# Two projection pairs of a gated-recurrence block: two of eight chunks by Strassen's scheme

## The chip, the cores and the metric

The kernel runs on one core of a Trainium2 chip. The metric is the device time of one execution in microseconds. A core has TensorE (PE in the profile, its weight loads PEld), VectorE (DVE), ScalarE (ACT), GpSimd (POOL), and queues for transfers that SyncE (SP) issues here. Each engine works through one queue in a fixed order, and waits for what other engines or transfers must have finished.

## The reference

One layer of a decoder block on 256 tokens of 2048 features, in fp32. Its first part is a projection of the normalized input, whose columns are cut into ten fields, each of them used in its own way:

```python
h = rmsnorm(x, norm_mix_g[i])
u = h @ w_in[i]                       # 2048 -> 12288
c_g, b_g, xa, za, q, fl, iv, og, ga, gb = jnp.split(u, split_idx, axis=-1)
ya = b_g * causal_dwconv3(c_g * xa, conv_w[i]) * jax.nn.silu(za)
...                                   # log_f and kk from fl
o = hgrn2_chunked(silu(q), kk, iv, log_f)      # a gated linear recurrence, 8 heads of 128
o = o * lax.rsqrt(jnp.mean(o * o, axis=-1, keepdims=True) + EPS)
yb = (o * hg_norm_g[i]) * jax.nn.silu(og)
m = jax.nn.sigmoid(ga) * (ya @ w_a_out[i]) + jax.nn.sigmoid(gb) * (yb @ w_b_out[i])
x = x + m @ w_o[i]
gate = jax.nn.sigmoid(rmsnorm(x, ple_norm_g[i]) @ w_ple_gate[i])
x = x + gate * (p[i] @ w_ple_proj[i])
return rmsnorm(x, final_norm_g)
```

The fields c, b, xa, za, q, f, iv and og are 1024 columns wide each, ga and gb 2048.

## The kernel before

**Numbers.** All products are made from fp32 values that are cut into a high part (hi, type fp32r) and the rest (lo). A product is three matmuls: hi by hi, hi by lo, lo by hi. The weights are cut on the chip: a transfer brings a chunk into a tile `raw` (three of them, line 106), ScalarE copies it to `whi` (line 151), VectorE subtracts to get `wlo` (line 152). `whi` and `wlo` are pairs of buffers, four in the pool `wp`. Such a pair is given back when PE has read it.

**Steps.** The work of PE is one list of steps (`steps`, line 181; `pos` is the step's number). A step takes one chunk of weights: 256 input features by 512 columns, so 128 x 1024 values in the tile. In a plain step both halves of a chunk meet both halves of the tokens, which makes 4 products, 12 matmuls of 512 columns (line 1147). A group of 8 steps makes 512 columns of a field. The columns of the projection go in two halves j = 0 and 1, and in each half the groups come in the order f, q, iv, og, c, xa, za, b (line 37). Ahead of them stand four steps for the projection of p, behind them the gates ga and gb with the output products A and B, then O, and last the gate PG of the last part. q of the first half is steps 12 to 19, iv 20 to 27.

**Strassen's scheme where it is used already.** The gates of j = 1 to 3 are taken in pairs (groups "GG", with the list `GATES`, line 42), and so is a pair of PG ("GP", with `LATE`). An entry (g, c) of such a list is two plain steps, chunks c and c + 1 of the pair's group g. An entry ("S", c) is a joint chunk: chunk c of both groups at once, in four parts. `combine_weights` (line 159) makes the sums and differences of the two groups' weights on VectorE, four parts are split, the second of them from the tile t2, half as wide, and `pair_products` (line 1157) makes seven products of 512 columns instead of the eight of two plain steps. It needs sums and differences of x as well, the forms (`forms` and `forms_of_x`, lines 722 to 757): xT is loaded once more for these chunks, scaled with the norm's gain, added on VectorE, split, and kept in tiles. PE gathers the results in eight PSUM banks, four named g and four s; `sums` (line 765) puts them together with six half-wide additions and one wide one on VectorE and one copy on ScalarE, as a generator that starts when the first joint chunk does.

**Epilogues.** What follows a group is a generator in `active`, and each step of PE's list moves every generator on by one (`advance`, line 1130). A half's f is evicted with the norm's scale (`scaled`, line 306), written to DRAM in four transfers, read back in one, and transposed on VectorE (`turned`, line 285); then come two sigmoids, four logarithm calls and a scan (lines 341 to 388). q is a sigmoid and a product in PSUM, turned in the same way (line 392). iv is one scaled eviction, og a sigmoid and a product, and behind og the recurrence `hgrn` of this half begins. The norm of x comes from squares of the tokens (`load_tokens`, `add_squares`, `norm_of_x`, lines 1033 to 1053), which are loaded from step 10 on and squared from step 13; so the f of the first half waits for it until step 17 (line 1241).

**What sets the order.** A scheduler writes the order of every engine's queue when the program is built; an instruction for a later step can stand ahead of one for an earlier step there. `issue_after` asks for a place behind the last split, and `keep_in_program_order` keeps a few instructions where the program has them. `ahead` (line 1138) says how many steps the splits are made ahead of PE: three, and one more where a stretch has additional buffers (`more`, line 207: pool `tmp2` around the gates; every fifth step takes its pair from there, line 140).

**Memory.** `tmp1` is the pool of the two halves: eight work tiles, the tiles v, qT, kT, b and og, and for the recurrence a pair X and the tiles a, both and aoff (line 430 and the lines behind it). yaT holds the turned result of branch A, one half of the tile for each j.

Of the kernel before, what the change touches and what calls it, by code (L numbers as in the profile page):

```python
# [9 lines left out]
F32 = mybir.dt.float32  # L10
F32R = mybir.dt.float32r
# [4 lines left out]
P = 128  # L16
# [7 lines left out]
CW = 512  # L24
# [15 lines left out]


GATES = ("S", 0), (0, 2), ("S", 1), (1, 2), ("S", 4), (0, 6), ("S", 5), (1, 6)
LATE = (0, 4), ("S", 0), (0, 6), ("S", 1), (1, 4), ("S", 2), ("S", 3), (1, 6)


# [6 lines left out]
def hybrid_kernel(ctx, tc, xT, x, pT, prm, gfin, masks, w_in, w_a, w_b, w_o, w_pg, w_pp, out):  # L52
# [10 lines left out]
    pools, closers = {}, {}  # L63
# [13 lines left out]
    state = {"tmp": "tmp1"}  # L77
# [3 lines left out]
    def nm(s):  # L81
        uid[0] += 1
        return f"{s}_{uid[0]}"
# [17 lines left out]
    half = {}  # L101
# [28 lines left out]
    def split(pos, c0=0, c1=2 * CW):  # L130
        part = part_of[pos]
        src = load(pos)[:, part % 2, :]
        if joint[pos]:

            src = load(pos)[:, part == 3, :]
            if part == 1:
                src, c1 = half[unit_of[pos]], CW

        pool, n = (pools["late"], 6) if (pos - state.get("late", len(steps))) % 10 < 6 and "late" in state else (wp, 4)
        if more(pos) and pos % (4 + MORE) < MORE:  # L140
            pool, n = pools[more(pos)], MORE
        if pos not in parts:
            parts[pos] = tuple(
                pool.tile([P, 2 * CW], F32R, tag=tag, bufs=n, name=nm(tag)) for tag in ("whi", "wlo")
            )
        hi, lo = parts[pos]
        s = slice(c0, c1)
        with ExitStack() as order:
            for i in state["before"].pop() if state.get("before") else ():
                order.enter_context(tc.issue_after(i))  # L150
            a = nc.scalar.activation(out=hi[:, s], in_=src[:, s], func=AF.Copy)  # L151
            v = nc.vector.tensor_tensor(  # L152
                out=lo[:, s], in0=src[:, s], in1=hi[:, s].bitcast(F32), op=ALU.subtract
            )
        state["splits"] = (a.ins, v.ins)
        if joint[pos] and part == 0:
            combine_weights(pos)

    def combine_weights(pos):

        b = load(pos).rearrange("p i (k c) -> p (i k) c", k=2)
        t2 = half[unit_of[pos]] = pools["tmp2" if pos in gates else "tmp3"].tile([P, CW], F32, tag="t2", bufs=2 if pos in gates else 1, name=nm("t2"))
        nc.vector.tensor_tensor(  # L163
            out=b[:, 0:4:3, :], in0=b[:, 0:3:2, :], in1=b[:, 3:4, :].to_broadcast([P, 2, CW]), op=ALU.subtract
        )
        nc.vector.tensor_tensor(out=t2, in0=b[:, 2, :], in1=b[:, 0, :], op=ALU.add)  # L166
        nc.vector.tensor_tensor(out=b[:, 1, :], in0=b[:, 1, :], in1=t2, op=ALU.subtract)
# [35 lines left out]
    of_kind = lambda *kinds: [pos for pos, (gi, c) in enumerate(steps) if groups[gi][0] in kinds]  # L203
    gates, late = of_kind("GG"), of_kind("PG")[0]
    gates = range(gates[0] - 12, gates[-1] + 9)

    def more(pos):

        return "tmp2" if pos in gates else None

    TOKENS, NORM = 10, 13
    FIRST = 6

    praw = t4()[:, : 2 * T]
# [180 lines left out]
        plain_times(psum, sg, qt)  # L395
        state["qT", j] = yield from turned(qt, 5, t4("qT", 1))

    def ep_iv(j, psum):
        v = t4("v", 1)
        scaled(psum, v)  # L400
        state["v", j] = v
        yield
# [316 lines left out]
        yield  # L719


    def forms(op, pool, tag, r, chunks):
# [11 lines left out]
        hi, lo = (pool.tile([P, 1024], F32R, tag=tag + x, bufs=len(chunks) // 2, name=nm(tag + x)) for x in "hl")  # L734
# [7 lines left out]
    def forms_of_x():  # L742

        joined = sorted(c for u, c in GATES if u == "S")
        for n in range(0, len(joined), 2):
            chunks = joined[n : n + 2]
            raw = t4()
            r = raw.rearrange("p (u k t) -> p u k t", u=2, k=2)
            for u in range(2):
                nc.sync.dma_start(out=r[:, u], in_=xT[:, 2 * chunks[u] : 2 * chunks[u] + 2, :])  # L750
            for u in range(2):
                yield
                for k in range(2):
                    h = r[:, u, k, :]
                    nc.scalar.activation(out=h, in_=h, func=AF.Identity, scale=gain(PRM_GMIX, 2 * chunks[u] + k))
            yield
            yield from forms("hT", pools["tmp2"], f"Sx{n}", r, chunks)
            yield

    def add(out, x, y):  # L760
# [32 lines left out]
    def ep_pair(j, e, left):  # L793
# [42 lines left out]
    def ep_o(j, psum):  # L836
# [18 lines left out]
        if j < 2:  # L855
# [8 lines left out]
            yield from forms("x1T", pools["tmp3"], f"So{j}", r, (2 * j, 2 * j + 1))  # L864
# [342 lines left out]
    for pos, (gi, c) in enumerate(steps[:last_group]):  # L1207
# [36 lines left out]
        if program:  # L1244
# [45 lines left out]
        if c == nch - 1:  # L1290
# [3 lines left out]
            if kind == "ga" and j == 0:  # L1294
                finish()
                second_part()
                active.append(forms_of_x())
# [106 lines left out]
```

## Time and profile before

Three runs took 815.71, 815.15 and 814.84 us, the median is 815.15.

| | |
|---|---|
| profiled execution | 814.94 us |
| its span on the core | 813.1 us |
| granted TensorE clock, mean | 0.997 |
| matmuls | 4196 |
| memory read | 173.97 MB |
| mean transfer rate over the span | 231 GB/s |

The span begins with the first instruction and ends with the last; what lies around it is 814.94 - 813.1 = 1.8 us. Times in the profile are microseconds from the start of the span. A row of the timeline is: start, busy time, engine, line, operation, result <- operands, number of instructions that were taken together, and in brackets an idle time before it and who ended it. A row of the groups is: busy time, count, share or idle time. L1147 is line 1147 of the kernel that is printed above, and tiles go by their names in it (the operand names begin with the result, so `wlo<-raw,whi` is a split's second half). A matmul shows 0.39 us from issue to end, but the next one is issued before that end.

### The profile page before, as it was taken

The numbers are of one execution on the slowest core, as the hardware profiler recorded it, in microseconds if no ns is written. First come the engines' busy times: TensorE is split into PE (matmuls) and PEld (weight loads), VectorE is DVE, ScalarE is ACT, GpSimd is POOL, SyncE is SP. The second block draws the span as 40 slices with busy tenths as digits, with TensorE's granted clock in tenths as the row PEclk, the third lists the DMA queues.
The fourth block names the chain that finished last, engine by engine and source line by source line (L and its number), as shares of the span: only waits on it lengthen the run. The fifth ranks groups of instructions, "written<-read, shape, count | busy, mean of one in ns | idle before, by whom it ended". The sixth has DMA issues, their size and how long they took to land.

```text
span 813.1 us, 10989 instructions
## 1 busy us (share of the span) xinstructions
PE 802.5 (99%) x4196; PEld 666.9 (82%) x4196; DVE 629.6 (77%) x742; ACT 465.2 (57%) x609; POOL 91.1 (11%) x74
## 2 busy tenths in 40 slices
PE   9999999999999999999999999999999999999995
PEld 7888888888888888888888888888888888888875
DVE  5747697967766488967767998998997657779996
ACT  7667475555555465565664555564564456665653
POOL 1000045400000055200001000100100000001012
PEclk9999999999999999999999999999999999999998
DMA  9979656747767555647764774774766687887442
GB/s 337 366 281 338 226 172 206 228 172 237 258 233 256 186 183 202 213 156 264 269 238 148 224 272 144 248 257 157 259 236 230 213 300 257 283 315 252 165 181 105
DMA packets 46709, 188.33 MB, mean 232 GB/s; under 512 B 5312, under 2 KB 14784, under 8 KB 31552
## 3 DMA queue, kind: packets, MB, share of 16 engines
q1 hardware_dynamic: 46512, 187.36, 66.6%
q8 instruction: 33, 0.54, 0.3%
q10 hardware_dynamic: 144, 0.26, 0.1%
q14 instruction: 20, 0.16, 0.1%
HBM read 173.97 MB, written 13.63 MB: 231 GB/s over the span
## 4 chain that ended last, share of the span: by engine, by line
PE 90%; DVE 5%; DMA 1%; issue 1%; ACT 1%; POOL 0%; ACTq 0%; POOLq 0%; DVEq 0%
PE g L1147 73%; PE g L1169 11%; PE s L1169 4%; DVE wlo L152 2%; DMA raw<-in_w_pg 1%; PE s L1147 1%; PE s L450 1%; DVE t L911 1%; DVE raw L163 1%; DMA raw<-in_w_pp 0%; DVE xs L912 0%; ACT whi L151 0%; DVE t L929 0%; DVE t L761 0%; DVE t L166 0%
## 5 line engine op out<-in xcount | busy, mean ns | idle before, releaser
L152 DVE TENSOR_TENSOR wlo<-raw,whi 128x1024 fp32r<-128x1024 f32 (+1 forms) x311 | 385.1, 1254 | 154.3 <-ACT whi L151 153.0
L151 ACT ACTIVATE whi<-raw 128x1024 fp32r<-128x1024 f32 (+1 forms) x311 | 320.8, 1049 | 251.1 <-PE g L1147 195.6
L1147 PE MATMUL g<-whi,xh 128*128 128x512 f32 (+1 forms) x656 | 251.8, 385 | 0.6 <-DVE t L761 0.6
L1147 PE MATMUL g<-wlo,xh 128*128 128x512 f32 (+1 forms) x656 | 251.9, 384 | 0.0
L1147 PE MATMUL g<-whi,xl 128*128 128x512 f32 (+1 forms) x656 | 251.7, 384 | 0.0
L1147 PEld LDWEIGHTS g<-whi,xh 128*128 128x128 f32 x656 | 123.3, 188 | 25.2 <-DVE t L761 1.0
L1147 PEld LDWEIGHTS g<-whi,xl 128*128 128x128 f32 x656 | 123.3, 188 | 24.5
L1147 PEld LDWEIGHTS g<-wlo,xh 128*128 128x128 f32 x656 | 123.3, 188 | 24.2
L1169 PE MATMUL g<-wlo,xh 128*128 128x512 f32 x160 | 62.2, 389 | 0.0
L1169 PE MATMUL g<-whi,xl 128*128 128x512 f32 x160 | 62.2, 389 | 0.0
L1169 PE MATMUL g<-whi,xh 128*128 128x512 f32 x160 | 62.1, 389 | 0.0
L1147 PE MATMUL g<-whi,mh 128*128 128x512 f32 x128 | 49.8, 389 | 0.0
L1147 PE MATMUL g<-wlo,mh 128*128 128x512 f32 x128 | 49.8, 389 | 0.0
L1147 PE MATMUL g<-whi,ml 128*128 128x512 f32 x128 | 49.6, 389 | 0.0
L151 ACT ACTIVATE whi<-t 128x512 fp32r<-128x512 f32 x16 | 10.1, 630 | 53.7 <-DVE t L166 53.7
L1169 PEld LDWEIGHTS g<-whi,xh 128*128 128x128 f32 x160 | 30.0, 188 | 6.2
L1169 PEld LDWEIGHTS g<-wlo,xh 128*128 128x128 f32 x160 | 30.0, 188 | 6.2
L1169 PEld LDWEIGHTS g<-whi,xl 128*128 128x128 f32 x160 | 30.0, 188 | 6.2
L824 POOL TENSOR_TENSOR t<-ga,gb 128x512 f32<-128x512 f32 x6 | 10.6, 1780 | 193.0 <-issue 118.1
L1147 PE MATMUL g<-whi,yaTh 128*128 128x512 f32 (+1 forms) x74 | 28.0, 385 | 0.5 <-ACT whi L151 0.5
L1147 PEld LDWEIGHTS g<-whi,mh 128*128 128x128 f32 x128 | 24.0, 188 | 5.0
L1147 PEld LDWEIGHTS g<-wlo,mh 128*128 128x128 f32 x128 | 24.0, 188 | 5.0
(250 smaller groups left out, 931.4 us busy)
## 6 DMA issues: line engine op xcount, KB each, us to landing
raw<-in_w_in SPq DMA_DIRECT2D x73, 1024.0 KB, 4.9
raw<-in_w_in SPq DMA_DIRECT2D x34, 512.0 KB, 6.0
raw<-in_w_o SPq DMA_DIRECT2D x16, 1024.0 KB, 6.0
raw<-in_w_pg SPq DMA_DIRECT2D x12, 1024.0 KB, 6.1
turn<-t SPq DMA_DIRECT2D x72, 128.0 KB, 2.6
t<-turn SPq DMA_DIRECT2D x18, 512.0 KB, 5.1
raw<-in_w_a SPq DMA_DIRECT2D x8, 1024.0 KB, 5.3
raw<-in_w_b SPq DMA_DIRECT2D x8, 1024.0 KB, 5.4
```

Of the source, the lines that this page charges most:

```text
L151: a = nc.scalar.activation(out=hi[:, s], in_=src[:, s], func=AF.Copy)
L152: v = nc.vector.tensor_tensor(out=lo[:, s], in0=src[:, s], in1=hi[:, s].bitcast(F32), op=ALU.subtract)
L163: nc.vector.tensor_tensor(out=b[:, 0:4:3, :], in0=b[:, 0:3:2, :], in1=b[:, 3:4, :].to_broadcast([P, 2, CW]), op=ALU.subtract)
L450: nc.tensor.matmul(heads(bk)[r, h, c if at is None else slice(at, at + 32)], key(h)[:, r], query(h)[:, c], start=True, stop=True, tile_pos ...
L824: (nc.vector if j == 3 else nc.gpsimd).tensor_tensor(out=spread(m, t), in0=blocks(ga[:, s]), in1=blocks(gb[:, s]), op=ALU.add)
L911: nc.vector.tensor_tensor(out=gt[:, s], in0=gt[:, s], in1=pw[:, s], op=ALU.mult)
L1147: nc.tensor.matmul(psum, a, b, start=first and n == 0, stop=last and n == 2)
L1169: nc.tensor.matmul(banks[name], x, y[:, s], start=k == total[name] and i == 0, stop=k == 1 and i == 2)
```

## The change

Two pairs of groups become joint groups: q and iv of the first half ("QV") and iv and og of the second ("VG"). In each, chunks 0 and 1 of the eight are joint, in the order of the new list `INNER`, and the other six of both groups stay plain. Steps 12 to 31 are now QV, everything behind stands four steps later, and behind VG eight.

- The forms of x for chunks 0 and 1 are made at step 9 (`FORMS`). They are kept in the second half of the two yaT tiles, which is free until branch A of the second half. Both pairs use the same forms; the gates keep theirs, which are made later.
- For the steps of both pairs, from three ahead of them on, every fifth step takes its weight buffers from the pair X of `tmp1`, and t2 is one of the tiles both and aoff. The splits go one step further ahead there.
- `ep_inner` puts the banks together with `sums` and then starts the epilogues of the two groups on the result in SBUF, in place of PSUM.
- The loads of the tokens are asked for in the branch for pairs too, since steps 12 and 13 are now there.

```diff
+INNER = (0, 2), (0, 4), ("S", 0), (0, 6), ("S", 1), (1, 2), (1, 4), (1, 6)
...
+        tags = "whi", "wlo"
         if more(pos) and pos % (4 + MORE) < MORE:
             pool, n = pools[more(pos)], MORE
+            if more(pos) == "tmp1":
+                tags, n = ("X", "X"), 2
...
+        pool, tag, n = ("tmp2", "t2", 2) if pos in gates else ("tmp3", "t2", 1)
+        if more(pos) == "tmp1":
+            pool, tag, n = "tmp1", ("both", "aoff")[unit_of[pos] // 2 % 2], 1
+        t2 = half[unit_of[pos]] = pools[pool].tile([P, CW], F32, tag=tag, bufs=n, name=nm("t2"))
...
-        if j == 0 or kind not in ("ga", "gb"):
+        if (kind, j) in (("q", 0), ("iv", 1)):
+            groups.append(({"q": "QV", "iv": "VG"}[kind], j, w_in, n, "hT", INNER))
+        elif (kind, j) in (("iv", 0), ("og", 1)):
+            continue
+        elif j == 0 or kind not in ("ga", "gb"):
             groups.append((kind, j, w_in, n, "hT"))
...
+    inner = [range(at[0] - 3, at[-1] + 1) for at in (of_kind("QV"), of_kind("VG"))]
...
-        return "tmp2" if pos in gates else None
+        return "tmp2" if pos in gates else "tmp1" if any(pos in at for at in inner) else None
 
-    TOKENS, NORM = 10, 13
+    TOKENS, NORM, FORMS = 10, 13, 9
...
-    def ep_iv(j, psum):
-        v = t4("v", 1)
+    def ep_iv(j, psum, v=None):
+        v = t4("v", 1) if v is None else v
...
+    def ep_inner(kinds, j, e, left):
+
+        def then(q, g):
+            halves = [g[:, A], g[:, B]]
+            after = ep_iv(j, halves, g) if kinds[q] == "iv" else epilogues[kinds[q]](j, halves)
+            next(after)
+            active.append(after)
+
+        yield from sums(e, left, lambda: tuple(t4("v", 1) if k == "iv" else t4() for k in kinds), then)
...
+        if pos == FORMS:
+            held = [x[:, 4:, :].rearrange("p k t -> p (k t)") for x in state["yaT"]]
+            active.append(forms_of_x(INNER, lambda n: lambda: held))
+            step(active[-1])
...
             if c == (min(n for n, (u, _) in enumerate(program) if u == "S"), 0):
-                active.append({"GG": ep_pair, "GP": ep_gates_late}[kind](j, banks, left))
+                if kind in ("QV", "VG"):
+                    active.append(ep_inner({"QV": ("q", "iv"), "VG": ("iv", "og")}[kind], j, banks, left))
+                else:
+                    active.append({"GG": ep_pair, "GP": ep_gates_late}[kind](j, banks, left))
             pair_products(c, program, opname)
             ask_ahead()
+            if 0 <= pos - TOKENS < 4:
+                load_tokens(pos - TOKENS)
```

`forms` and `forms_of_x` take the list and a function that gives the tiles, and else do what they did. Lines of the changed kernel lie up to 35 further down than those of the kernel before.

More of the change, by code (lines that the diff above doesn't have):

```diff
@@ L139, in split @@
         pool, n = (pools["late"], 6) if (pos - state.get("late", len(steps))) % 10 < 6 and "late" in state else (wp, 4)
+        tags = "whi", "wlo"
         if more(pos) and pos % (4 + MORE) < MORE:
             pool, n = pools[more(pos)], MORE
+            if more(pos) == "tmp1":
+                tags, n = ("X", "X"), 2
         if pos not in parts:
             parts[pos] = tuple(
-                pool.tile([P, 2 * CW], F32R, tag=tag, bufs=n, name=nm(tag)) for tag in ("whi", "wlo")
+                pool.tile([P, 2 * CW], F32R, tag=tag, bufs=n, name=nm("w" + x)) for tag, x in zip(tags, ("hi", "lo"))
             )
@@ L161, in combine_weights @@
         b = load(pos).rearrange("p i (k c) -> p (i k) c", k=2)
-        t2 = half[unit_of[pos]] = pools["tmp2" if pos in gates else "tmp3"].tile([P, CW], F32, tag="t2", bufs=2 if pos in gates else 1, name=nm("t2"))
+        pool, tag, n = ("tmp2", "t2", 2) if pos in gates else ("tmp3", "t2", 1)
+        if more(pos) == "tmp1":
+            pool, tag, n = "tmp1", ("both", "aoff")[unit_of[pos] // 2 % 2], 1
+        t2 = half[unit_of[pos]] = pools[pool].tile([P, CW], F32, tag=tag, bufs=n, name=nm("t2"))
         nc.vector.tensor_tensor(
@@ L719, in ep_gb, with forms @@
         yield
-    def forms(op, pool, tag, r, chunks):
+    def forms(op, made, r, chunks):
         f = t4()
@@ L733, in forms @@
         yield
-        hi, lo = (pool.tile([P, 1024], F32R, tag=tag + x, bufs=len(chunks) // 2, name=nm(tag + x)) for x in "hl")
+        hi, lo = made()
         nc.scalar.activation(out=hi, in_=f, func=AF.Copy)
@@ L740, in forms, with form_tiles, forms_of_x @@
                 state["S", op, chunks[u], i] = hi[:, s], lo[:, s]
-    def forms_of_x():
-        joined = sorted(c for u, c in GATES if u == "S")
+    def form_tiles(pool, tag):
+        return lambda: tuple(pool.tile([P, 1024], F32R, tag=tag + x, bufs=1, name=nm(tag + x)) for x in "hl")
+    def forms_of_x(program, made):
+        joined = sorted(c for u, c in program if u == "S")
         for n in range(0, len(joined), 2):
@@ L756, in forms_of_x @@
             yield
-            yield from forms("hT", pools["tmp2"], f"Sx{n}", r, chunks)
+            yield from forms("hT", made(n), r, chunks)
             yield
@@ L863, in ep_o @@
             r = x1.rearrange("p (u k t) -> p u k t", u=2, k=2)
-            yield from forms("x1T", pools["tmp3"], f"So{j}", r, (2 * j, 2 * j + 1))
+            yield from forms("x1T", form_tiles(pools["tmp3"], f"So{j}"), r, (2 * j, 2 * j + 1))
             return
@@ L1296, in hybrid_kernel @@
                 second_part()
-                active.append(forms_of_x())
+                active.append(forms_of_x(GATES, lambda n: form_tiles(pools["tmp2"], f"Sx{n}")))
                 step(active[-1])
```

## The prediction

> **What bounds the kernel now.** I read the page's busy times first, then the chain that ended last, then the waits, then single stretches.
>
> ```profile
> span 813.1 us, 10989 instructions
> PE 802.5 (99%) x4196; PEld 666.9 (82%) x4196; DVE 629.6 (77%) x742; ACT 465.2 (57%) x609; POOL 91.1 (11%) x74
> PE 90%; DVE 5%; DMA 1%; issue 1%; ACT 1%; POOL 0%; ACTq 0%; POOLq 0%; DVEq 0%
> ```
> ```profile
> 16.70 119.68 PE g L1147 x528
> 547.20 21.76 PE g L1147 x96
> ```
> ```profile
> ACT whi L151 <- PE g L1147: 195.6, 129, 4.4
> PEld g L1147 <- DVE t L761: 1.0, 1, 1.0
> ```
>
> The chain is 90% PE. Its pieces give the price of a matmul: 119.68 / 528 = 21.76 / 96 = 0.2267 us. (A matmul's own row says 0.39 us: that is issue to end of a pipelined instruction, not its price.) The page's PE share alone would not prove that PE is the bound, but the waits do: ACT's splits stand 195.6 us waiting until PE gives a weight buffer back, and the one wait of PE's weight loads on DVE is 1.0 us. So time goes by the count of matmuls, as long as the splits keep ahead. They do by a margin that differs from place to place (columns: window, length, then busy us of PE, PEld, DVE, ACT, POOL, the granted clock, DMA share, GB/s):
>
> ```profile
> 40.00:60.00 20.00, 20.00 (x90) 16.57 (x89) 8.57 (x10) 12.17 (x17) 0.78 (x2) 1.00 0.73 293
> 60.00:80.00 20.00, 20.00 (x89) 16.54 (x89) 14.38 (x19) 13.90 (x17) 0.00 (x0) 1.00 0.94 324
> 240.00:260.00 20.00, 20.00 (x90) 16.56 (x89) 15.55 (x16) 11.12 (x13) 1.96 (x1) 1.00 0.75 253
> 260.00:280.00 20.00, 20.00 (x90) 16.54 (x89) 8.58 (x7) 9.42 (x10) 0.00 (x0) 1.00 0.61 206
> 460.00:480.00 20.00, 20.00 (x90) 16.57 (x89) 18.69 (x20) 12.75 (x14) 0.00 (x0) 1.00 0.63 225
> ```
>
> The first two windows hold q and iv of the first half, the next two iv and og of the second, the last a gate pair that is already done by Strassen: there DVE is 93% busy and PE still runs without a hole. The granted clock is 1.00 in all.
>
> The Trainium skill ("Perfetto Trace Analysis", section "Identifying the Most-Contended Engine") holds matmul busy time to be a bad measure and would judge TensorE's headroom by the busy share of its weight loads. That is 82% here, which read literally leaves 18% of room. But in every window above it is 16.5 of 20, also where nothing but matmuls runs, so 83% is what a full PE shows in this kernel, and I take PE as full.
>
> **The gain.** A Strassen chunk takes 7 products of three matmuls (21) where two plain parts take 24. Two chunks in each of two pairs: 12 matmuls fewer, 12 x 0.2267 = 2.72 us. That is all the change can give: 812.4 us.
>
> **What is added, and how much DVE has left.** Durations on DVE back to back, from a gate pair, with the scan and the copy of f's epilogue:
>
> ```profile
> 443.44 1.28 DVE L819 TENSOR_TENSOR gb<-gb,g 128x512 f32<-128x512 f32 x2
> 450.04 1.22 DVE L163 TENSOR_TENSOR raw<-raw 128x1024 f32<-128x1024 f32 x1
> 451.29 0.69 DVE L166 TENSOR_TENSOR t<-raw 128x512 f32<-128x512 f32 x1
> 452.02 0.69 DVE L167 TENSOR_TENSOR raw<-raw,t 128x512 f32<-128x512 f32 x1
> 452.77 0.69 DVE L152 TENSOR_TENSOR wlo<-t,whi 128x512 fp32r<-128x512 f32 x1
> 453.92 5.76 DVE L152 TENSOR_TENSOR wlo<-raw,whi 128x1024 fp32r<-128x1024 f32 x5 [0.47 <-ACT whi L151]
> 459.72 1.23 DVE L163 TENSOR_TENSOR raw<-raw 128x1024 f32<-128x1024 f32 x1
> ```
> ```profile
> 83.06 2.28 DVE L380 TENSOR_TENSOR_SCAN b<-carry,t 128x1024 f32<-128x1024 f32 x1
> 85.26 1.20 DVE L152 TENSOR_TENSOR wlo<-raw,whi 128x1024 fp32r<-128x1024 f32 x1
> 86.38 1.08 DVE L385 COPY tot<-b 128x8 f32<-128x8 f32 x1
> 87.37 0.15 DVE L386 TENSOR_TENSOR tot<-b,lfl 128x8 f32<-128x8 f32 x1
> ```
>
> One wide subtraction costs 5.76/5 = 1.15 and a half-wide one 0.64. A joint chunk needs 3 x 1.15 + 0.65 for its splits and 1.25 + 0.73 + 0.75 for the combination, 6.8 us, in 4.76 us of PE (21 matmuls); two plain parts need 2.3 in 5.44. The two chunks of a pair add about 9 us to DVE, the sums six half-wide additions and one wide (5 us), the forms of x some 3 us, once. So the first stretch (23 us busy in 40) comes to about 40 in 42, the second (24) to about 38 in 42. On average it fits; what decides is the order. I therefore took the built order of the changed kernel and summed each queue along it: every instruction starts when its queue is free and the tile or buffer that the program makes it wait for is there. The same sum over the first gate pair of the kernel as it is gives no hole in PE and meets DVE's starts above to 0.2 to 1.1 us, so I trust it to about half a microsecond per place.
>
> **The second pair (iv, og), from 240.98.**
>
> ```profile
> 240.98 0.39 PE L1147 MATMUL g<-whi,xh 128*128 128x512 f32 x1
> ```
>
> Counted from there, plain parts one to four end at 2.7, 5.4, 8.2 and 10.9; the first joint chunk ends at 15.6, the next two plain parts at 21.1. ACT's queue has the split of the first chunk's fourth part ahead of its second and third. This one uses the borrowed X pair, which the third plain part holds until 8.1, while DVE has finished the combination at 6.1 plus 0.6 and stands still until ACT's hi is there at 9.2. From 9.2 on DVE has in one row: three subtractions (1.15 + 0.6 + 1.15), f's scan (2.2), one more (1.15), the copies (1.06), two (1.15 + 1.27), the second combination (1.27 + 0.73 + 0.68), 0.6, q's transpose (1.3), and then the lo of the second chunk's third part (1.23): 24.8. PE wants it nine matmuls into that chunk, at 21.1 + 10 x 0.2267 = 23.35. **Stall: 1.45 us.** Nothing behind it is late again.
>
> **The first pair (q, iv), from 38.30.**
>
> ```profile
> 38.30 0.39 PE L1147 MATMUL g<-whi,xh 128*128 128x512 f32 x1
> ```
> ```profile
> 49.38 1.06 ACT L151 ACTIVATE whi<-raw 128x1024 fp32r<-128x1024 f32 x1 [1.66 <-PE g L1147]
> 50.35 1.04 ACT L1041 ACTIVATE t<-t 128x1024 f32<-128x1024 f32 x1
> 58.24 1.27 ACT L308 ACTIVATE t<-g,r1r 128x512 f32<-128x512 f32 x2 [1.32 <-POOL r1r L271]
> ```
>
> Here the built order of PE already pushes the products with forms of x behind plain ones. The hi of the forms stands on ACT behind a split that PE releases at 12.45 and a square of the tokens: 12.45 + 0.97 + 1.04 + 1.06 = 15.55 against 15.4 wanted; the lo follows by 1.25. About 0.3 us lost. The matmul that reads that lo also gives back the buffer for the second chunk's first split: 17.3 (with the 0.3), ACT 1.06, DVE 1.23, the combination 1.27 + 1.27 less the overlap + 0.73 + 0.6, and the fourth part's lo at 23.5; PE wants it at 22.3. Another 1.2, and 0.2 behind it. **Stall: 1.7 us.**
>
> **The first half's f.** Its epilogue needs the norm of x, whose squares now stand on ACT among the splits of the second chunk: eviction at about 62.8 instead of 58.24. Then f goes out to DRAM and back:
>
> ```profile
> 59.54 1.78 SPq L294 DMA_DIRECT2D turn<-t  x4
> 63.96 0.33 SPq L296 DMA_DIRECT2D t<-turn  x1
> ```
> ```profile
> t<-turn SPq DMA_DIRECT2D x1, 512.0 KB, 5.8
> ```
> ```profile
> 69.94 1.24 DVE L300 STREAM_TRANSPOSE t<-t 128x1024 f32<-128x1024 f32 x1
> ```
>
> 58.24 to 63.96 + 5.8 = 69.8 is 11.5 us, so about 74.4. DVE reaches that transpose at 73.4 and stands behind it; every split behind it waits too. ACT's two sigmoids, the two halves of q's sigmoid, the table load and three logarithms (5.5 us) come before og's first split, which is at 81.2, its lo at 83.5; PE wants it two matmuls into og, at 38.30 + 186 x 0.2267 + 1.7 + 0.45 = 82.6. **Stall: 0.9 us.** This is the least certain term: it is 0 with a lag of 10.5 us and 2 with 12.6. The ends are the two lags that the trace shows, 69.8 - 58.24 above and q's, which took 12.5 from 64.81 (first DMA of the turn) to 73.70 + 3.6 = 77.3 (the read's landing) behind f's:
>
> ```profile
> 64.81 3.20 SPq L294 DMA_DIRECT2D turn<-t  x4
> 73.70 0.34 SPq L296 DMA_DIRECT2D t<-turn  x1
> ```
> ```profile
> t<-turn SPq DMA_DIRECT2D x1, 512.0 KB, 3.6
> ```
>
> I take f's own, since the load between its parts is the same. The 512 KB of xT for the forms take the place of a token load in SP's queue, so S0's weights land as before and the tokens one load later; the squares alone wait for those. I cost it at 0, at worst 512 KB at the 324 GB/s of the second window above, 1.6 us. Also 0: the borrowed tiles X, both, aoff and the second half of yaT (hgrn's users of the first half end before the second pair, yaT's writer comes after it), the s banks (free in both stretches), and hgrn of the second half, whose y comes 2.7 us later on DVE while PE's order gives it 2.7 us more.
>
> **Sum.** -2.72 + 1.45 + 1.7 + 0.9 = +1.3 us. Against the profiled execution (814.94 us, its span 813.1) 816.2; the median of the runs shown is 815.15, which gives 816.4. 0.2% of it, 1.6 us, is about what a measurement of this kernel can tell from no change.
>
> **Rivals.**
> 1. Everything is hidden, as in the gate pairs: 812.4. For it: 18.69 of 20 busy on DVE at 460 to 480 without a hole. Against: there the parts are split in order, no scan, squares or transposes stand between them. It needs all three stalls to be wrong.
> 2. f's turn is in time (lag below 10.5), the two other stalls stay: 815.6.
> 3. Slower: f comes back from DRAM later than 74.4, because the 1 MB load that stands between its write and its read goes first. Each us beyond costs one us of PE; with q's lag, 12.5 and more, and token loads one place later, 2 to 3 us: 818 to 819. It decides from a lag of about 12.
> 4. PE was not the bound, and fewer matmuls give nothing back: the stalls would be hidden in that room as well or cost 4 us in full, up to 819. Waits of 195.6 us on PE speak against it. This is the way the skill's rule on weight loads would have it.
>
> **How the numbers follow.** Forecast (816.4) 0.44, rival 2 0.20, rival 3 0.23, rival 1 0.10, rival 4 0.03. The forecast's own range is 815.7 to 817.2, so a third of it lies above the 816.8 where "slower" begins; rivals 2 lies within, 3 and 4 are slower, 1 is faster: faster 0.10, same 0.50, slower 0.40. For 8 in 10 the range leaves out the far ends of rivals 1 and 3: 813.6 to 818.5.
>
> **What would show it.** PE's count falls by 12 matmuls. PE, now without a hole from 17 to 780, gets holes near 54 to 56 (0.3), 62 (1.2), 82 (0.9) and 264 (1.4), and a wait of PE on DVE's lo at L156 appears among the waits. DVE idles some 2.5 us near 248 on ACT's hi. og of the first half, which 186 matmuls after 38.30 would begin at 80.5 without a hole, begins at 80.5 + 1.7 = 82.2, and its first product with a lo stands until 83.5. Wrong, if f's transpose starts before 73.5 or after 75.5, or if xT lands after 45.

## The result, and the profile after

The changed kernel took 818.4 us (median of 6 runs, 818.17 to 820.12), the kernel before 815.22 (median of 6). The ratio is 1.0044, 95% interval 1.0034 to 1.0054: slower by 0.44%. That is 3.2 us by the medians and 3.6 by the ratio, where +1.3 us had been forecast and no measurable change was given the largest chance (0.50). The profiled execution of the changed kernel took 818.25 us, its span is 816.5. The page's first lines and its chain:

```profile
span 816.5 us, 11044 instructions
PE 803.0 (98%) x4184; PEld 664.6 (81%) x4184; DVE 656.7 (80%) x781; ACT 473.9 (58%) x624; POOL 89.5 (11%) x74
...
PE 81%; DVE 7%; issue 4%; ACT 3%; DMA 3%; POOL 0%; SPq 0%; ACTq 0%; POOLq 0%; DVEq 0%
```

PE has its 12 matmuls fewer (4184 against 4196), and its share of the chain fell from 90% to 81%: PE waits. The view of waits says for whom (engine, line <- releaser: us in total, times, longest). L156 is the split's lo, L155 its hi, L1195 the products of a pair, L1173 those of plain steps:

```profile
PE s L1195 <- DVE wlo L156: 2.0, 3, 1.0
...
PE g L1173 <- DVE wlo L156: 0.5, 1, 0.5
PE s L1195 <- ACT whi L155: 0.4, 1, 0.4
PE g L1173 <- ACT whi L155: 0.3, 1, 0.3
```

The first three rows did not stand in the view before. The last did (0.5 us there); it is a matmul at 5.37 us, far ahead of the pairs. The four windows that the prediction shows of before look like this now (window, length, then busy us of PE, PEld, DVE, ACT, POOL, the clock, DMA share, GB/s):

```profile
40.00:60.00 20.00, 20.00 (x88) 16.00 (x88) 14.79 (x17) 12.34 (x18) 0.53 (x1) 1.00 0.97 390
60.00:80.00 20.00, 18.90 (x81) 14.62 (x80) 17.36 (x24) 15.46 (x20) 1.15 (x2) 1.00 0.64 217
240.00:260.00 20.00, 20.00 (x90) 16.58 (x89) 15.61 (x20) 11.52 (x14) 2.96 (x3) 1.00 0.55 174
260.00:280.00 20.00, 18.59 (x79) 14.23 (x78) 19.01 (x20) 10.83 (x13) 0.69 (x1) 1.00 0.64 225
```

PE started 81 and 79 matmuls in the second and the fourth window where it had started 89 and 90. DVE rose to 17.36 and 19.01 of 20 us there, and the granted clock stayed at 1.00.

A better measure than a wait's length is the time from one matmul's start to the next, less the 0.227 us that it takes when nothing is in the way. Summed over a place (only where it is over 0.06 us longer), this gives the "holes" of the table below. In the changed kernel they are 2.26 us in the first pair (53 to 64 us), 1.09 at the first matmuls of og (82 to 84), 2.50 in the second pair (261 to 269), and 0.2 more than before at the one old hole near the end. 2.26 + 1.09 + 2.50 + 0.2 - 2.72 = +3.3 us; PE's last matmul starts 3.5 us later than before (807.63 against 804.14).

### The profile page after: what moved, and what is told of

It reads as the page before. It is cut to its first block, busy times and chain, and to the rows that moved or that the text cites. A ratio compares the mean times of both kernels' runs of the same rounds, so it can differ in the third digit from the quotient of the medians.

```text
span 816.5 us, 11044 instructions
## 1 busy us (share of the span) xinstructions
PE 803.0 (98%) x4184; PEld 664.6 (81%) x4184; DVE 656.7 (80%) x781; ACT 473.9 (58%) x624; POOL 89.5 (11%) x74
## 4 chain that ended last, share of the span: by engine, by line
PE 81%; DVE 7%; issue 4%; ACT 3%; DMA 3%; POOL 0%; SPq 0%; ACTq 0%; POOLq 0%; DVEq 0%
PE g L1173 59%; PE g L1195 16%; PE s L1195 5%; DVE wlo L156 3%; ACT whi L155 1%; DMA t<-in_xT 1%; DMA raw<-in_w_in 1%; PE s L462 1%; DMA raw<-in_w_pg 1%; DVE t L937 1%; DVE raw L170 1%; DMA raw<-in_w_pp 1%; ACT t L905 0%; DVE t L777 0%; DVE xs L938 0%
## 5 line engine op out<-in xcount | busy, mean ns | idle before, releaser
L156 DVE TENSOR_TENSOR wlo<-raw,whi 128x1024 fp32r<-128x1024 f32 (+1 forms) x315 | 389.6, 1255 | 132.4 <-ACT whi L155 131.2
L155 ACT ACTIVATE whi<-raw 128x1024 fp32r<-128x1024 f32 (+1 forms) x315 | 323.4, 1048 | 236.5 <-PE g L1173 161.6
L1173 PE MATMUL g<-whi,xh 128*128 128x512 f32 (+1 forms) x528 | 202.9, 385 | 0.8 <-DVE t L777 0.8
L1173 PE MATMUL g<-wlo,xh 128*128 128x512 f32 (+1 forms) x528 | 202.5, 384 | 0.5 <-DVE wlo L156 0.5
L1173 PE MATMUL g<-whi,xl 128*128 128x512 f32 (+1 forms) x528 | 202.2, 383 | 0.0
L1173 PEld LDWEIGHTS g<-whi,xh 128*128 128x128 f32 x528 | 99.3, 188 | 20.8 <-DVE t L777 1.2
L1173 PEld LDWEIGHTS g<-wlo,xh 128*128 128x128 f32 x528 | 99.3, 188 | 20.0 <-DVE wlo L156 1.0
L1173 PEld LDWEIGHTS g<-whi,xl 128*128 128x128 f32 x528 | 99.3, 188 | 19.4
L1195 PE MATMUL g<-wlo,xh 128*128 128x512 f32 x264 | 103.0, 390 | 0.0
L1195 PE MATMUL g<-whi,xl 128*128 128x512 f32 x264 | 102.9, 390 | 0.0
L1195 PE MATMUL g<-whi,xh 128*128 128x512 f32 x264 | 102.1, 390 | 0.0
L1195 PEld LDWEIGHTS g<-wlo,xh 128*128 128x128 f32 x264 | 49.6, 188 | 10.9 <-DVE wlo L156 0.6
L1195 PEld LDWEIGHTS g<-whi,xh 128*128 128x128 f32 x264 | 49.6, 188 | 10.3
L1195 PEld LDWEIGHTS g<-whi,xl 128*128 128x128 f32 x264 | 49.6, 188 | 10.2
L1173 PE MATMUL g<-wlo,mh 128*128 128x512 f32 x128 | 49.9, 390 | 0.0
L1173 PE MATMUL g<-whi,mh 128*128 128x512 f32 x128 | 49.9, 390 | 0.0
L1173 PE MATMUL g<-whi,ml 128*128 128x512 f32 x128 | 49.7, 390 | 0.0
L155 ACT ACTIVATE whi<-t 128x512 fp32r<-128x512 f32 x20 | 12.6, 628 | 61.2 <-DVE t L173 61.2
L1173 PE MATMUL g<-whi,yaTh 128*128 128x512 f32 (+1 forms) x74 | 28.0, 385 | 0.3 <-ACT whi L155 0.3
L1173 PEld LDWEIGHTS g<-wlo,mh 128*128 128x128 f32 x128 | 24.0, 188 | 5.0
L1173 PEld LDWEIGHTS g<-whi,ml 128*128 128x128 f32 x128 | 24.1, 188 | 5.0
```

Source lines behind the costliest of these rows:

```text
L156: v = nc.vector.tensor_tensor(out=lo[:, s], in0=src[:, s], in1=hi[:, s].bitcast(F32), op=ALU.subtract)
L1173: nc.tensor.matmul(psum, a, b, start=first and n == 0, stop=last and n == 2)
L1195: nc.tensor.matmul(banks[name], x, y[:, s], start=k == total[name] and i == 0, stop=k == 1 and i == 2)
```

## The experiments

Every kernel was timed beside the kernel before on the same chip. Holes are those of the one profiled execution, medians and ratios those of all runs (us; "last" is the start of PE's last matmul, 804.14 before).

| run | first pair | og | second pair | last | profiled execution | median | ratio to before, 95% |
|---|---|---|---|---|---|---|---|
| changed kernel | 2.26 | 1.09 | 2.50 | 807.63 | 818.25 | 818.40 | 1.0034 to 1.0054 |
| e1 first pair alone | 2.27 | 1.45 | 0 | 806.77 | 817.38 | 818.59 | 1.0021 to 1.0047 |
| e2 second pair alone | 0 | 0 | 2.48 | 807.16 | 817.78 | 817.99 | 1.0023 to 1.0043 |
| e3 subtractions on DVE | 2.26 | 1.72 | 0.64 | 808.53 | 819.15 | 817.04 | 1.0011 to 1.0028 |
| e4 X one step earlier | 2.27 | 2.32 | 2.19 | 808.65 | 819.51 | 819.05 | 1.0024 to 1.0050 |
| e5 forms and tokens early | 0.54 | 1.29 | 4.09 | 807.37 | 818.01 | 816.38 | 1.0004 to 1.0022 |
| e6 e3 and e4 | 2.25 | 0.80 | 0.41 | 805.19 | 815.88 | 816.53 | 1.0007 to 1.0024 |
| e7 all edits | 0.56 | 0.49 | 0.11 | 802.83 | 813.72 | 814.07 | 0.9974 to 0.9992 |
| e8 second pair alone, e3, e4 | 0 | 0 | 0 | 803.00 | 813.62 | 814.00 | 0.9977 to 0.9995 |
| e9 forms early | 1.15 | 1.84 | 2.50 | 807.59 | 818.49 | 818.02 | 1.0021 to 1.0045 |
| e10 tokens early | 3.09 | 0.17 | 2.49 | 807.63 | 818.74 | 819.43 | 1.0039 to 1.0069 |
| e11 e7, tokens at step 8 | 1.22 | 2.14 | 0.40 | 805.21 | 815.89 | 813.66 | 0.9978 to 0.9998 |

The holes of the two pairs repeat to a few hundredths of a us wherever the code around them is the same (2.25 to 2.27 in five kernels, 2.48 to 2.50 in four). One execution is an exception: the 4.09 of e5 holds 1.6 us of a lower granted clock, see the section on the hardware. The hole at og does not repeat (0.80 to 2.32 in the five kernels that are alike up to it). It is one source of the scatter, but not the only one: the runs of e2 and e8, whose profiled executions have no hole at og, lie up to 3.1 and 3.5 us apart as well, and what scatters there is open.

### One pair at a time (e1, e2)

```diff
-        if (kind, j) in (("q", 0), ("iv", 1)):
+        if (kind, j) == ("q", 0):                  # e1; e2 keeps ("iv", 1)
...
-    TOKENS, NORM, FORMS = 10, 13, 9
+    TOKENS, NORM, FORMS = 10, 13, 66               # e2 only
```

> Only q and iv of the first half are a pair; iv and og of the second are plain again, and the gates take their additional buffers at the same steps of theirs as before. Theory (the time is the count of matmuls plus PE's holes, and each hole belongs to its own pair): 6 matmuls fewer, -1.36 us, and the holes that the changed kernel shows between 53 and 64 us (2.27) and at og of the first half (1.09) stay as they are: +2.0 us against the kernel before. The holes near 262 to 269 are gone. Rival (the products with forms are dearer in themselves, by place and bank, whatever stands around them): both pairs cost the same, half of the 3.2 us, +1.6 us, with holes after 260 or without.

> Only iv and og of the second half are a pair; q and iv of the first are plain, and the forms of x are made later, at step 66 and not at 9. The pair and the gates take their additional buffers at the same steps of theirs as in the changed kernel. Theory: -1.36 us, holes of 2.5 us between 261 and 269 (less the 2.1 us by which the pair starts earlier), 0.2 at the end: +1.1 to +1.4 us against the kernel before; no hole from 38 to 110. Rival as in the first run: +1.6 us. Second rival (the holes of the second pair come from what the first one has put late): no hole, -1.4 us.

In both kernels the gates take their additional buffers at the same steps of theirs as in the kernel before (for e2 the expectation says as in the changed kernel); no kernel here has a hole around the gates. Each pair keeps its own holes and has none at the other's place, so the holes are local, and the second pair's don't come from the first. The first pair is dearer by 2.27 + 1.45 - 1.36 = 2.4 us (2.63 by the last matmul; 1.7 to 3.8 by the ratio, where 2.0 was expected). The second is 2.48 - 1.36 = 1.1 us dearer by its holes, as expected, but the kernel was 1.9 to 3.5 us slower. 1.15 us of that are one matmul far behind the pair, for which PE waited on nothing that the profile shows; the section on the hardware comes back to it. By their holes the two add up to the changed kernel; by their times they don't (about 2.8 and 2.7 us by the ratios, against 3.6 for both), so the times hold something that a pair doesn't bring.

### The second pair: who makes DVE late (e3, e4, e6)

The prediction put the second pair's hole down to the borrowed pair X. The wait is there. DVE's timeline of the changed kernel (start, busy, engine, line, operation; in brackets the idle time before it), then ACT's and POOL's rows that go with it:

```profile
248.21 0.69 DVE L174 TENSOR_TENSOR raw<-raw,t 128x512 f32<-128x512 f32 x1
252.32 1.23 DVE L156 TENSOR_TENSOR wlo<-raw,whi 128x1024 fp32r<-128x1024 f32 x1 [3.41 <-ACT whi L155]
...
255.20 2.29 DVE L392 TENSOR_TENSOR_SCAN b<-carry,t 128x1024 f32<-128x1024 f32 x1
257.40 1.20 DVE L156 TENSOR_TENSOR wlo<-raw,whi 128x1024 fp32r<-128x1024 f32 x1
258.51 1.08 DVE L397 COPY tot<-b 128x8 f32<-128x8 f32 x1
259.51 0.15 DVE L398 TENSOR_TENSOR tot<-b,lfl 128x8 f32<-128x8 f32 x1
259.59 3.32 DVE L156 TENSOR_TENSOR wlo<-raw,whi 128x1024 fp32r<-128x1024 f32 x2
262.94 1.23 DVE L170 TENSOR_TENSOR raw<-raw 128x1024 f32<-128x1024 f32 x1
...
267.57 4.63 DVE L156 TENSOR_TENSOR wlo<-raw,whi 128x1024 fp32r<-128x1024 f32 x4
```
```profile
251.22 1.06 ACT L155 ACTIVATE whi<-raw 128x1024 fp32r<-128x1024 f32 x1 [3.73 <-PE g L1195]
```
```profile
257.56 3.13 POOL L516 TENSOR_TENSOR t<-b 128x512 f32<-128x512 f32 x2 [2.84 <-DVE b L392]
```

DVE stands 3.41 us at 249 until ACT has its hi at 252.3, and ACT waited 3.73 us for PE to give X back. But two things behind it are not what they seem: a copy of 8 elements takes 1.08 us, and two splits that follow each other without a gap take 3.32 us where the four at 267.57 take 4.63, 1.16 each. Over just these two rows POOL works on two subtractions of the second half's recurrence (L516). They belong to a later stage, but need nothing more than the scan's b, and POOL's queue was empty. The first of the two alone:

```profile
257.56 2.00 POOL L516 TENSOR_TENSOR t<-b 128x512 f32<-128x512 f32 x1 [2.84 <-DVE b L392]
```

It begins while DVE is at the split of 257.40, which takes its usual 1.20, and ends at 259.56; the copy, begun at 258.51, ends just behind it. The second ends at 260.69, and the split of 259.59 goes on for 1.1 us after that, about the length of a whole split. e3 puts these two on DVE, e4 moves X, e6 does both.

```diff
-                nc.gpsimd.tensor_tensor(out=er, in0=br, in1=ref, op=ALU.subtract)
+                (nc.vector if j and B > 8 else nc.gpsimd).tensor_tensor(out=er, in0=br, in1=ref, op=ALU.subtract)   # e3, e6
...
-        if more(pos) and pos % (4 + MORE) < MORE:
+        if more(pos) and (pos + (0 if more(pos) == "tmp2" else 1 if pos > 40 else 0)) % (4 + MORE) < MORE:         # e4, e6
```

> The changed kernel, with the first two subtractions of the second half's recurrence on VectorE and not on GpSimd (the same numbers, 2 x 0.69 us more on VectorE). Theory (while GpSimd works on its tensor, VectorE stands: a split of 2.18 us in place of 1.23 at 259.6, and the 8-element copy of 1.08): those two are short again, VectorE's row is some 2 us earlier, the holes of the second pair go from 2.5 to 0.6 to 1.3 us, the time is 1.2 to 2 us below the changed kernel, 816.4 to 817.2. Rival (VectorE has too much work there, 27.4 of 32 us, and the long split is only a coincidence): the two more instructions make it later, 818.4 to 819.8.

> The changed kernel; the second pair takes the borrowed pair X one step earlier (steps 4, 9, 14 and 19 in place of 5, 10, 15 and 20 of each 20), so that no fourth part of a joint chunk waits for it. Theory of the prediction (that wait is what makes VectorE late): VectorE's idle 3.41 us at 249 goes and the holes of the second pair with it, up to 2.5 us, 816 to 817. Theory with GpSimd's lock as a second cause: the idle time goes, and about 2 us of holes stay, 817.8 to 818.0. Rival (VectorE is short of time in the stretch as a whole): 818.4, the same holes.

> The changed kernel with both edits to the second pair, the two subtractions on VectorE and the pair X one step earlier. Theory (two causes that add up, GpSimd's work and the wait for X): no hole from 240 to 290, so 2.5 us below the changed kernel, 815.9. By the prediction's theory alone (X is the cause) it would equal the run with the other phase, 818 to 819; by GpSimd alone the run with the subtractions on VectorE, some 0.7 us of hole left, 816.6.

With the subtractions off POOL (e3), DVE's rows at the same place are:

```profile
259.05 1.20 DVE L156 TENSOR_TENSOR wlo<-raw,whi 128x1024 fp32r<-128x1024 f32 x1
260.17 0.17 DVE L397 COPY tot<-b 128x8 f32<-128x8 f32 x1
...
260.32 2.36 DVE L156 TENSOR_TENSOR wlo<-raw,whi 128x1024 fp32r<-128x1024 f32 x2
```

The copy takes 0.17 in place of 1.08 and the two splits 2.36 in place of 3.32: 1.87 us that DVE had stood still while POOL worked. The holes fall from 2.50 to 0.64, the median to 817.04, inside what was expected. DVE's own work at this place was the same: the two subtractions that it took over run at 296 and 304, behind the pair. So the rival that DVE is short of time there is out; what two more instructions inside the pair would cost was not seen.

The Trainium skill ("SBUF — State Buffer", section "Who interferes with whom") says that a VectorE instruction with two SBUF inputs, or in a two-port mode, and a GpSimd instruction that reads SBUF exclude each other for the whole instruction. The rows agree: the copy and the split end one copy and about one split behind the end of a subtraction, as if they had not run beside it at all.

With X moved alone (e4) DVE's idle time is gone, and still the holes are 2.19:

```profile
250.73 0.69 DVE L174 TENSOR_TENSOR raw<-raw,t 128x512 f32<-128x512 f32 x1
251.45 0.69 DVE L156 TENSOR_TENSOR wlo<-t,whi 128x512 fp32r<-128x512 f32 x1
253.79 2.36 DVE L156 TENSOR_TENSOR wlo<-raw,whi 128x1024 fp32r<-128x1024 f32 x2 [1.64 <-ACT whi L155]
...
259.38 1.08 DVE L397 COPY tot<-b 128x8 f32<-128x8 f32 x1
260.38 0.15 DVE L398 TENSOR_TENSOR tot<-b,lfl 128x8 f32<-128x8 f32 x1
260.46 3.31 DVE L156 TENSOR_TENSOR wlo<-raw,whi 128x1024 fp32r<-128x1024 f32 x2
```

Part of the waiting moved to 252 (1.64 us), and copy and splits have POOL's price again. So X is worth 0.3 us of holes alone, POOL 1.9: about 2 us of holes stay, as the theory with a second cause had it. The time of e4, 819.05, lies above all three of its forecasts, and its interval overlaps that of the changed kernel; og's hole was 2.32 in the profiled execution, the slowest of the five, and is not known for the others. Both edits (e6) leave 0.41 of holes, and 816.53 in place of the 815.9 expected for no hole at all. By time alone e6 can't be told from e3 (817.04, the intervals overlap, and 816.6 had been expected for POOL as the only cause); that X adds anything is read from the holes.

### The first pair (e5, e9, e10)

```diff
-    TOKENS, NORM, FORMS = 10, 13, 9
+    TOKENS, NORM, FORMS = 9, 13, 7        # e5;  e9: 10, 13, 7;  e10: 9, 13, 9
```

> The changed kernel with the forms of x begun at step 7 in place of 9 and the token loads asked for at step 9 in place of 10; nothing else. Theory (the first pair's holes and the late f come from the order on ScalarE: hi of the forms behind a split, squares among the splits of the second joint chunk): the squares end 4.8 us earlier, f is evicted 2.2 us earlier, the holes from 53 to 64 go from 2.27 to about 0.45 us and og's hole at 83 is gone (1.1 to 2.3 in the runs so far): 814.5 to 816. Rival (VectorE is short of time in the first pair as a whole, 34.5 of 44.3 us busy): the holes stay, 818 to 819. Second rival (f's way through DRAM sets og's hole by traffic, whatever the time of eviction): the first holes go, og's stays, 816.5.

> The changed kernel with the forms begun at step 7 in place of 9, the token loads as they were. Theory (the place of a few instructions on ScalarE makes the first pair's holes): the hole at 53 is gone, those at 60 to 64 fall from 1.9 to about 1.0 us; f is evicted 0.7 us earlier, so og's hole is some 0.7 us smaller: 816.7 to 817.6. Rival (tokens alone made the difference in the run with both): as the changed kernel, 818.4.

> The changed kernel with the token loads asked for at step 9 in place of 10, the forms as they were. Theory: the loads of the tokens now stand before those of xT, the squares come into the way of other splits, and the first pair's holes are not fewer but about 0.9 us more, 3.1 us; f is evicted 0.75 us earlier. 818 to 819.3. Rival (an earlier norm is what counts, since it makes f early): 816.5 to 817.5.

ACT's rows of the changed kernel show what the prediction had summed: the hi of the forms (L747) behind a square, the last square among the splits of the second joint chunk, f's eviction after it:

```profile
52.72 1.05 ACT L747 ACTIVATE yaTh<-t 128x1024 fp32r<-128x1024 f32 x1
...
60.24 1.04 ACT L1067 ACTIVATE t<-t 128x1024 f32<-128x1024 f32 x1
...
63.30 1.27 ACT L320 ACTIVATE t<-g,r1r 128x512 f32<-128x512 f32 x2 [0.46 <-POOL r1r L283]
```

Nothing is taken away in these three kernels, only the order changes, and the first pair's holes go from 2.26 to 1.15 with early forms, to 3.09 with early tokens, to 0.54 with both. e10 was expected at 3.1; its 819.43 lies just above the 818 to 819.3. So it is the order on ACT and in SP's queue, not DVE's load, which is much the same in all four (34.2 to 35.1 us busy from 38.3 to 82.6). e5 reached 816.38, above the 814.5 to 816 expected and next to the 816.5 of its second rival, by which og's hole stays whenever f is evicted. It did stay (1.29): f was evicted at 60.64, 2.7 us earlier, but its transpose began only 1.6 us earlier (73.33), and PE, with fewer holes, came to og 1.8 us earlier too. e9 is 818.02, above its 816.7 to 817.6; its og hole was 1.84. The 0.17 of e10 goes with PE coming to og late, after 3.09 us of holes.

og's hole is the step that scatters. Two executions with the same code up to there, the changed kernel and e4 (DVE's transpose of f, ACT's split before it, and f's read from DRAM, us to landing):

```profile
74.94 1.24 DVE L312 STREAM_TRANSPOSE t<-t 128x1024 f32<-128x1024 f32 x1
```
```profile
72.70 2.01 ACT L155 ACTIVATE whi<-raw 128x1024 fp32r<-128x1024 f32 x2 [3.85 <-DMA raw<-in_w_in]
```
```profile
t<-turn SPq DMA_DIRECT2D x1, 512.0 KB, 4.9
```
```profile
76.06 1.24 DVE L312 STREAM_TRANSPOSE t<-t 128x1024 f32<-128x1024 f32 x1
```
```profile
73.83 2.01 ACT L155 ACTIVATE whi<-raw 128x1024 fp32r<-128x1024 f32 x2 [5.10 <-DMA raw<-in_w_in]
```
```profile
t<-turn SPq DMA_DIRECT2D x1, 512.0 KB, 6.0
```

In e4 f lands 0.9 us later (69.00 + 6.0 = 75.0 against 69.22 + 4.9 = 74.1), the weights that ACT waits for 1.1 us later, the transpose starts 1.12 us later, and og's hole is 2.32 in place of 1.09. Neither transpose has an idle time before it: f had landed, and DVE was at a split whose weights ACT had waited for, until 72.70 and 73.83. From eviction to transpose it takes 11.6 us here, 12.9 there, and 12.2 in e3, where the transpose does wait for f.

### All edits, and the second pair alone (e7, e8, e11)

```diff
# e7: both edits of e6, FORMS = 7, TOKENS = 9, and in the first pair
+        if more(pos) and (pos + (0 if more(pos) == "tmp2" else 1 if pos > 40 else 4)) % (4 + MORE) < MORE:
# e8: both edits of e6 on e2 (X there moves two steps, see below);   e11: e7 with TOKENS, NORM, FORMS = 8, 14, 7
```

> All edits together: two subtractions on VectorE, X one step earlier in the second pair and one step later in the first, forms at step 7, tokens from step 9. Theory: the 12 matmuls fewer are worth 2.72 us once PE has no holes for them; about 0.2 us left in the first pair, 0.2 at the end, none in the second: 2.3 us below the kernel before, 812.6 to 813.6. Rival (something else than the holes makes the pairs dear, or the holes come back at another place): 815 or more.

> Only the pair of the second half (iv and og), forms at step 66, two subtractions on VectorE, X one step earlier: what the second run had, with its two causes taken away. Theory: 1.36 us below the kernel before, 813.7 to 814.3, as there is no hole but the one at the end (0.1 to 0.2 longer). Rival (the excess of the second run over its holes, about 1 us at one matmul of 352 us for which no engine is waited, comes with the pair): 815 to 815.5.

> As the kernel with all edits (both pairs cured), but the tokens from step 8 and their squares from step 14. Theory (f's way back from DRAM sets og's hole by its time of eviction): f is evicted 4.8 us earlier than there, og's hole of 0.5 us and the small ones of the first pair are gone: 0.5 to 1 us below it, 812.8 to 813.5. Rival (the rest of the loss against 2.72 us isn't in the holes): 814, as there.

e7 and e8 are faster than the kernel before, by 0.17% (e7, 0.08 to 0.26) and 0.14% (e8, 0.05 to 0.23). e8 is what 6 matmuls are worth when no hole is added: 804.14 - 803.00 = 1.14 us by the last matmul (1.36 less the end's 0.2), 814.00 where 813.7 to 814.3 was expected. But the same `+ 1` moves X two steps earlier there, not one as the expectation says, since the pair begins at step 84 and not at 88 and the offset counts from the step's number. So e8 is not quite e6's second pair alone, and its missing hole (0.41 in e6) may come from that. e7's page and PE's waits:

```profile
span 811.6 us, 11039 instructions
```
```profile
PE g L1173 <- DVE t L777: 0.6, 1, 0.6
PE g L1173 <- ACT whi L155: 0.5, 1, 0.5
PE g L1173 <- DVE wlo L156: 0.2, 1, 0.2
```

The wait for sums (L777) is the old one near the end, the wait for ACT is the one at the kernel's start, the last row is og's, and the waits of the pairs (L1195) have gone from the list. 1.2 us of holes are left, and e7 gets 1.3 us of its 2.72 (some 0.2 are in no hole that was counted). It missed the 812.6 to 813.6 expected: the first pair, even so, gives back nearly all that it gains. e11 evicts f 4.1 us earlier than e7 (56.30 against 60.42). Seven of its runs took 813.06 to 813.75 and four 815.00 to 816.95; the profiled one is one of the four. It has 1.22 us of holes in the first pair and 2.14 at og, ahead of which ACT waited 4.54 us for weights from DRAM (until 73.48). So in this execution the time of f's eviction did not set og's hole, against the theory; what set it was not followed further. Its median of 813.66 is a little above the 812.8 to 813.5 expected, and is not settled to be better than e7's.

## Why the prediction was wrong, point by point

By the holes the +1.3 us became +3.3: 0.56 more in the first pair, 0.19 at og, 1.05 in the second pair and 0.2 near the end. The measured 818.4 lies just inside the range of 813.6 to 818.5, whose upper end was put there for rival 3; that rival's cause is not the main one, so this is luck.

- **PE bounds the kernel, and a matmul is worth 0.2267 us:** right. With the holes gone, 6 matmuls gave 1.14 us (e8). Rival 4, by which fewer matmuls give nothing, is out, and with it the reading of the Trainium skill's rule by which 82% weight-load time leaves headroom: the kernel before and e8 both stand at 82%, and six matmuls fewer still gave their time back.
- **The first pair, "Stall: 1.7 us":** the two places and their order are right (forms at 53 to 55, the second joint chunk at 60 to 64), the size was 2.26. A price that was not in the sum gives the rest: a hole is followed by one matmul that takes 0.34 us to the next start in place of 0.227. There are five such restarts here, 5 x 0.11 = 0.55.
- **The first half's f, "Stall: 0.9 us":** 1.09 in the profiled execution, two restarts of 0.11 among it, with the transpose at 74.94 (74.4 had been forecast), and 0.80 to 2.32 in others with the same code up to there. The lag of f was nearly right (10.8 us from eviction to landing, for the 11.5 assumed); not in the sum was that the weight load beside it can land as late, and holds DVE's queue ahead of the transpose. The other end of the lags is not on the same basis: q's 12.5 is counted from the first write, and f's, counted so, was 10.2 (59.54 to 69.8).
- **The second pair, "Stall: 1.45 us. Nothing behind it is late again":** this is the step that failed; it was 2.50. The prediction priced "the copies (1.06)" as DVE's own work, from the copy's row of before, 1.08 us, and has no term for POOL. By e3 0.17 of such a row is the copy; the rest goes with POOL, whose subtraction ran from 85.48 to 87.43 beside the row that the prediction shows. So one subtraction was in the sum under another name. In the changed kernel two of them fall into the pair, not one as before (251.28 to 253.24 there), and the second held a split for another 0.96 us. Counted from the pair's start at 243.09, DVE was done with the copies after 16.5 us, as the sum has it, with the two splits behind them after 19.8 (18.9 in the sum), and with the second chunk's third lo after 25.7, at 268.80 (24.8 in the sum). PE wanted that lo after 23.4 us, as forecast, so 2.39 of the 2.50 lie ahead of the matmul at 268.85, the shorter holes from 261 to 268 among them; the rest is the restart behind it. The wait for X, which the prediction named as the cause, is real, but alone it is worth 0.3 us.
- **Costed at 0:** the borrowed tiles both and aoff held up no matmul that the waits show, and ACT scaled xT from 41.56, before the 45 given as the limit. The old hole near the end grew by 0.2 us; why was not tried.
- **Rivals:** "slower, because f comes back late" (818 to 819, from a lag of 12) lies where the changed kernel came out, and e4's profiled execution shows some of it (transpose at 76.06, og's hole 2.32), but it is not the main cause: without og's 1.09 the changed kernel's last matmul would still start 2.4 us later than before. "Everything is hidden" (812.4) was not reached with all edits either (814.07).

## What to carry to other kernels

Before a stage gets more work on an engine that "fits on average", write down that engine's queue in order, and put into the sum each engine that can hold it up, also one whose instructions belong to a later stage but have their inputs already: an idle queue runs them at once. A short operation that takes long (8 elements, 1.08 us) is a wait in disguise, and the other engines' rows of that time show on whom. Count holes in PE by their number too, since each costs a restart, and cure the order before judging the arithmetic: the same 7/8 scheme was 0.44% slower or 0.17% faster by the place of a few instructions.

## What the runs showed of the hardware

**The restart.** PE's rows of the changed kernel at the last hole of the second pair:

```profile
266.43 0.50 PE L1195 MATMUL s<-wlo,yaTh 128*128 128x512 f32 x1 [0.22 <-DVE wlo L156]
266.76 0.40 PE L1195 MATMUL s<-whi,yaTl 128*128 128x512 f32 x1
267.59 0.50 PE L1195 MATMUL s<-whi,yaTh 128*128 128x512 f32 x1 [0.43 <-ACT whi L155]
268.85 0.50 PE L1195 MATMUL s<-wlo,yaTh 128*128 128x512 f32 x1 [0.76 <-DVE wlo L156]
269.19 0.40 PE L1195 MATMUL s<-whi,yaTl 128*128 128x512 f32 x1
```

A matmul that had to wait shows 0.50 us in place of 0.39, and the next starts 0.34 after it (268.85 to 269.19). Its weight load begins with it, at 268.85, while the load for the matmul of 269.65 begins at 269.43, one matmul ahead. That the difference of 0.11 us is the part of the load that is then not hidden is inferred, not tested; a load's own row shows 0.19. The Trainium skill ("TensorE: Matmul & The Clock Gate", section "LDWEIGHTS (loading the stationary operand)") gives a load columns / 1.2 ns, so 107 ns for 128 as an estimate, near that difference.

**Half the clock for a moment.** In the profiled execution of e5, and not in the changed kernel's with the same holes, the granted clock fell at the last of them (e5, then the changed kernel, then a matmul of e5; the windows' columns as above):

```profile
267.00:271.00 4.00, 3.72 (x9) 3.00 (x10) 4.00 (x5) 3.35 (x4) 0.00 (x0) 0.57 0.37 104
```
```profile
267.00:271.00 4.00, 2.81 (x11) 1.99 (x11) 3.96 (x5) 4.00 (x6) 0.00 (x0) 1.00 0.05 8
```
```profile
268.30 0.63 PE L1195 MATMUL g<-whi,xh 128*128 128x512 f32 x1
```

Six matmuls in a row took 0.43 us from start to start, which made e5's second pair 4.09 in place of 2.50. That the holes brought the clock down is not shown, since the changed kernel had the same holes and kept 1.00. The Trainium skill (the same page, section "What's actually happening") lets the clock fall after an idle window of some 3.4 us; no matmul here started more than 1.3 us behind the one before it, so that window alone does not explain this execution.

**A matmul that waits for nothing.** In e2 PE stood before one matmul, with no releaser in the profile; one transfer of instructions falls into that stretch (e2's timeline; then the row of the transfers' view from 349 to 354):

```profile
353.66 0.39 PE L1173 MATMUL g<-wlo,xh 128*128 128x512 f32 x1 [0.98 <-issue]
```
```profile
q8 instruction: 1, 0.02, 1.2%
```

e3 has the like at 356.36 (0.75 us). In the changed kernel such a transfer comes between 351 and 356 too, without a hole of that size. Whether the transfer has to do with it was not tried, and how much of e2's time it makes in its other runs stays open.
